# The rows that stream through the later feed-forwards start at other addresses

## Chip, core and metric

One core of a Trainium2 chip runs the whole network in one launch. The metric is the device time of that launch in microseconds (us); the time of the kernel before is the median of three executions, and one further execution was profiled.

## What is computed

The model has two layers over 256 latent tokens and 256 context tokens of width 1024. Each layer is a half-step feed-forward, a token mixer (a two-directional SSD in layer 0, grid pooling in layer 1) and a second half-step feed-forward. The stretch that matters here is the feed-forward on the latent tokens alone, which runs three times: after the mixer of layer 0, before the mixer of layer 1 and after it.

```python
def swiglu(u, wg, wu, wd):
    return (jax.nn.silu(u @ wg) * (u @ wu)) @ wd
...
x = x + 0.5 * m[:, 8] * swiglu(modulate(x, norm_g[i, 2], m[:, 6], m[:, 7]),
                               ffn_w_gate[i, 1], ffn_w_up[i, 1], ffn_w_down[i, 1])
```

The inner width is 2816, that is 22 blocks of 128. All of it is float32.

## The kernel before, in words

Every float32 product is made of three passes through TensorE (`mm3`, L201): a weight tile is split into a high part `hi` and a low remainder `lo`, the activations likewise, and the passes are hi by high rows (L202), lo by high rows (L203) and hi by low rows (L204). The weight block of 128 x 128 is loaded into the array, and the activations are streamed past it: 128 partitions, and along each partition a run of 256 float32 values, one for each token. These runs are the "streamed rows" of this document. Every pass has a weight load of its own.

The last three feed-forwards are one function, `ffn` (L935), called at L1007, L1009 and L1068. Here they are called the first, second and third sub-layer. Each has 22 gate and 22 up tiles (output bank `gu`, rows from the tiles `vh` and `vl`), eight cells of three passes each, and then eight down tiles (output bank `dn`, rows from the 22 pairs `hh` and `hl`), 22 cells of three passes each. In the first NV = 3 gate and up tiles the run is 258 values, since two bias columns ride along while the norm is still being found; from the fourth on (`settle`, L953) and in the down product it is 256.

`vh` and `vl` are [128, 8, 320] tiles of the pool `vp`, one run of 320 values (TS, L335) for each of the eight blocks, of which the slice `c` (L344) picks 258. `Scaled` (L337) makes that slice, and takes its first column from the queue VOFF (L934); it is called four times without tiles of its own, for the first sub-layer (L1003), the second, the pooling mixer and the third (L987, L1042). `hh` and `hl` are 44 tiles of 1024 bytes in a pool that is opened anew in each sub-layer; in front of them `skip` (L110) may reserve some bytes, by the queue HOFF (L995). In the kernel before all offsets are zero.

The layout fixes where these stand. A tile's place is a multiple of 32 bytes: `epsc` (L124), a column of 4 bytes, is followed by `mhalf` 32 bytes on. `vh` begins 145,024 bytes into each partition, `vl` 155,264, the first `hh` 180,864: all three leave 128 when divided by 256, and since a run of `vh` is 1280 bytes and a tile `hh` 1024, so does every streamed run of the three sub-layers. Every weight tile `hi` and `lo` leaves 192, and since a block in it is 512 bytes, so does every loaded block. In the SSD mixer the streamed rows `uh` and `ul` leave 192; in the pooling product `pq` the roles are exchanged, so that the weights' tiles are streamed (192) and `vh` is loaded (128).

The weights come by DMA from SyncE's queue into a ring of six raw tiles (`wsplit`, L190); ScalarE makes `hi`, VectorE `lo`. VectorE also does the modulation products of later layers (L141), whose pace is set at L1002. The order on each engine is the order of the program; the framework puts in the semaphores.

Of the kernel before, what the change touches and what calls it, by code (L numbers as in the profile page):

```python
# [62 lines left out]
def tile_hybrid_backbone(  # L63
# [867 lines left out]
    work = st3.enter_context(tc.tile_pool(name="fw1", bufs=1))  # L931
    adap.append(st3.enter_context(tc.tile_pool(name="ada1", bufs=2)))

    HOFF, VOFF = deque((0, 0, 0)), deque((0, 0, 0, 0))  # L934
    def ffn(l, s, sub, nrm, vec, nxt_vec):  # L935

        ws = [wsplit(wgu[l, s, i % 2, i // 2]) for i in range(2 * NV)]
# [223 lines left out]
```

## Time and profile before

| | us |
|---|---|
| median of three runs | 1321.36 |
| the three runs | 1317.01, 1322.84, 1321.36 |
| the profiled execution | 1321.0 |
| its span, first to last instruction | 1319.1 |
| TensorE busy in the span | 1254.4 |

The profiled execution's own time is 1.9 us over its span, which is the work around it. In the views, PE is TensorE's matmul and PEld its weight load. A matmul's duration in the views (0.28 us for a 256-value run) holds a tail that overlaps the next one; how fast the engine goes is read from the distance of two starts, or from how many matmuls a stretch holds in which the engine is never idle.

### The profile page before, as it was taken

What the parts mean: (1) busy time and instruction counts of PE and PEld (TensorE: products, weight loads), DVE (VectorE), ACT (ScalarE), POOL (GpSimd) and SP (SyncE); (2) the same over time, 40 slices, a digit from 0 to 9 for tenths busy, and PEclk for the clock granted to TensorE, in tenths of its full rate; (3) what the DMA queues carried; (4) which work ended last, traced back from release to release, by engine and by line L of the source; (5) the groups of instructions that cost most, each with busy time, mean ns of one, the idle gap of its engine ahead of it and who ended that gap; (6) DMA issues with size and microseconds to landing.
All of it is one profiled execution on the core that took longest, in us unless ns stands there. A gap on an engine that the chain in (4) does not pass through costs nothing.

```text
span 1319.1 us, 21138 instructions
## 1 busy us (share of the span) xinstructions
PE 1254.4 (95%) x8246; PEld 1120.4 (85%) x8246; DVE 992.4 (75%) x1568; ACT 597.6 (45%) x1023; POOL 177.1 (13%) x121
## 2 busy tenths in 40 slices
PE   4999999989999979899988999999999999999997
PEld 2788888878888757777776999999999999999997
DVE  6889987863367878998997988767987566865553
ACT  3243222222235766655453654544544445745441
POOL 4100000000003141434264300000200000200000
PEclk7999999999999979999999999999999999999999
DMA  9488788872223413434343598777798565275661
GB/s 365 146 303 262 251 329 316 294 268 88 79 89 105 178 48 115 153 119 152 132 153 111 192 332 318 265 214 245 260 318 286 176 192 176 94 242 192 183 186 33
DMA packets 74996, 262.46 MB, mean 199 GB/s; under 512 B 8272, under 2 KB 10768, under 8 KB 73872
## 3 DMA queue, kind: packets, MB, share of 16 engines
q1 hardware_dynamic: 74896, 261.11, 58.5%
q8 instruction: 65, 1.06, 0.3%
q14 instruction: 35, 0.29, 0.1%
HBM read 259.96 MB, written 1.11 MB: 198 GB/s over the span
## 4 chain that ended last, share of the span: by engine, by line
PE 62%; DVE 18%; DMA 8%; issue 4%; ACT 3%; POOL 3%; SPq 1%; POOLq 0%; DVEq 0%; ACTq 0%
PE gu L204 11%; PE gu L202 11%; PE gu L203 11%; PE dn L202 6%; PE dn L204 6%; PE dn L203 6%; DMA adaw<-in_ada_dram 6%; DVE junk L141 6%; DVE lo L198 3%; DVE ca L595 2%; POOL em L708 1%; PE py L768 1%; DMA em<-acd 1%; PE po L772 1%; PE ip L204 1%
## 5 line engine op out<-in xcount | busy, mean ns | idle before, releaser
L198 DVE TENSOR_TENSOR lo<-raw,hi 128x1024 fp32r<-128x1024 f32 (+1 forms) x312 | 386.7, 1242 | 149.8 <-ACT hi L196 149.1
L196 ACT ACTIVATE hi<-raw 128x1024 fp32r<-128x1024 f32 (+1 forms) x333 | 342.8, 1037 | 307.6 <-PE dn L204 123.6
L202 PE MATMUL gu<-vh,hi 128*128 128x256 f32 (+1 forms) x1056 | 295.3, 280 | 3.3 <-DVE sg L967 2.6
L204 PE MATMUL gu<-vl,hi 128*128 128x256 f32 (+1 forms) x1056 | 294.8, 280 | 1.0 <-DVE vl L957 1.0
L203 PE MATMUL gu<-vh,lo 128*128 128x256 f32 (+1 forms) x1056 | 294.9, 279 | 0.0
L141 DVE SCALAR_TENSOR_TENSOR junk<-adaw,cb 128x1024 bf16<-128x1024 f32 x152 | 183.7, 1222 | 48.3 <-DMA adaw<-in_ada_dram 47.6
L202 PE MATMUL dn<-hh,hi 128*128 128x256 f32 (+1 forms) x704 | 215.7, 306 | 4.2 <-DVE x L329 4.2
L204 PE MATMUL dn<-hl,hi 128*128 128x256 f32 (+1 forms) x704 | 215.8, 307 | 0.0
L203 PE MATMUL dn<-hh,lo 128*128 128x256 f32 (+1 forms) x704 | 215.7, 306 | 0.0
L202 PEld LDWEIGHTS gu<-vh,hi 128*128 128x128 f32 x1056 | 199.4, 189 | 3.7 <-DVE sg L967 2.8
L204 PEld LDWEIGHTS gu<-vl,hi 128*128 128x128 f32 x1056 | 200.5, 190 | 1.5 <-DVE vl L957 1.4
L203 PEld LDWEIGHTS gu<-vh,lo 128*128 128x128 f32 x1056 | 199.3, 189 | 0.0
L202 PEld LDWEIGHTS dn<-hh,hi 128*128 128x128 f32 x704 | 132.6, 188 | 11.6 <-issue 4.6
L203 PE MATMUL gu<-uh,lo 128*128 128x512 f32 x352 | 137.8, 392 | 1.9 <-POOL lo L198 1.9
L204 PEld LDWEIGHTS dn<-hl,hi 128*128 128x128 f32 x704 | 133.3, 189 | 6.9
L202 PE MATMUL gu<-uh,hi 128*128 128x512 f32 x352 | 138.6, 394 | 0.0
L203 PEld LDWEIGHTS dn<-hh,lo 128*128 128x128 f32 x704 | 132.5, 188 | 7.0
L204 PE MATMUL gu<-ul,hi 128*128 128x512 f32 x352 | 136.4, 392 | 1.6 <-DVE ul L470 1.4
L243 POOL TENSOR_TENSOR rs<-ms,mhalf 128x2 f32<-128x2 f32 (+1 forms) x6 | 5.4, 904 | 915.9 <-DVE ms L241 915.9
L296 ACT ACTIVATE hh<-hf 128x256 fp32r<-128x256 f32 (+1 forms) x88 | 40.9, 465 | 88.9 <-DVE hf L325 87.0
L203 PEld LDWEIGHTS gu<-uh,lo 128*128 128x128 f32 x352 | 66.4, 189 | 16.2 <-POOL lo L198 2.4
L204 PEld LDWEIGHTS gu<-ul,hi 128*128 128x128 f32 x352 | 65.9, 188 | 15.9 <-DVE ul L470 2.3
(266 smaller groups left out, 1897.5 us busy)
## 6 DMA issues: line engine op xcount, KB each, us to landing
raw<-in_wgu_dram SPq DMA_DIRECT2D x176, 512.0 KB, 4.6
adaw<-in_ada_dram SPq DMA_DIRECT2D x136, 512.0 KB, 5.2
raw<-in_wd_dram SPq DMA_DIRECT2D x64, 512.0 KB, 3.7
raw<-in_win_dram SPq DMA_DIRECT2D x25, 512.0 KB, 3.6
raw<-in_wd_dram SPq DMA_DIRECT2D x32, 384.0 KB, 3.4
raw<-in_wz_dram SPq DMA_DIRECT2D x16, 512.0 KB, 3.6
em<-acd SPq DMA_DIRECT2D x8, 1024.0 KB, 4.8
raw<-in_wout_dram SPq DMA_DIRECT2D x16, 512.0 KB, 4.6
```

What stands on the lines that cost most here:

```text
L141: v.scalar_tensor_tensor(junk, w, 1.0, cb2[i], op0=ALU.mult, op1=ALU.mult, accum_out=M[l][:, t, i : i + 1])
L196: sc.activation(hi[:, 0:n], r[:, 0:n], AF.Copy)
L198: (sub or v).tensor_tensor(lo[:, 0:n], r[:, 0:n], f32(hi[:, 0:n]), op=ALU.subtract)
L202: pe.matmul(out, wh, xh, start=start, stop=False)
L203: pe.matmul(out, wl, xh, start=False, stop=False)
L204: pe.matmul(out, wh, xl, start=False, stop=stop)
L243: gp.tensor_tensor(r, ms, mhalf[:, 0:n], op=ALU.pow)
L296: sc.activation(a, h, AF.Copy)
L595: v.scalar_tensor_tensor(avw[:, :, lo:hi], ov[:, :, lo + off : hi + off], hw[:, 5 * t + k : 5 * t + k + 1], avw[:, :, lo:hi], op0=ALU.mult ...
L708: gp.tensor_tensor(EM[0][:, :, j, :], EM[0][:, :, j, :], EM[1][:, :, j, :], op=ALU.add)
L768: pe.matmul(py[:, hc], EM[0][:, h, j, :], xl[:, hc], start=True, stop=True)
L772: pe.matmul(po, CT[:, j * P : (j + 1) * P], hin[d][0 if j == d else 1], start=True, stop=True)
```

## The change

The two queues of offsets get values, in columns of 4 bytes. No instruction is added, removed or reordered.

```diff
-    HOFF, VOFF = deque((0, 0, 0)), deque((0, 0, 0, 0))
+    HOFF, VOFF = deque((4, 60, 8)), deque((4, 60, 0, 8))
+
     def ffn(l, s, sub, nrm, vec, nxt_vec):
```

In `vh` and `vl` the slice begins 4, 60 and 8 columns in: 16, 240 and 32 bytes. 240 bytes higher is 16 lower, counted in blocks of 256. The pooling mixer's slice stays at 0. In front of `hh` and `hl` the pool gets a reserve of 16, 240 and 32 bytes.

## Rows read from the trace of the kernel before

**Rows 1.** The page: busy time of TensorE; then the chain of waits, 720 us on.
```profile
span 1319.1 us, 21138 instructions
...
PE 1254.4 (95%) x8246; PEld 1120.4 (85%) x8246; DVE 992.4 (75%) x1568; ACT 597.6 (45%) x1023; POOL 177.1 (13%) x121
...
by line: PE gu L204 19.7%; PE gu L202 19.7%; PE gu L203 19.6%; PE dn L202 10.1%; PE dn L204 10.1%; PE dn L203 10.1%; DMA adaw<-in_ada_dram 0.9%; issue 0.7%; PE op L204 0.7%; PE op L203 0.7%; PE op L202 0.7%; PE pq L202 0.6%; DVE x L978 0.5%
```

**Rows 2.** Groups by shape, the whole span: matmuls of 256 and 258, count, mean ns.
```profile
L204 PE MATMUL gu<-vl,hi 128*128 128x256 f32 x912 | 253.6, 278 | 1.0 <-DVE vl L957 1.0
...
L203 PE MATMUL dn<-hh,lo 128*128 128x256 f32 x528 | 146.6, 278 | 0.0
...
L203 PE MATMUL gu<-vh,lo 128*128 128x258 f32 x144 | 41.6, 291 | 0.0
```

**Rows 3.** PE alone in pairs of stretches: first, second, third sub-layer (gate, then down).
```profile
core 0: us, PE busy (x), PEclk, DMA share, GB/s
770.00:850.00 80.00, 80.00 (x709) 1.00 0.90 317
860.00:915.00 55.00, 55.00 (x488) 1.00 0.70 219
950.00:1030.00 80.00, 80.00 (x681) 1.00 0.86 299
1050.00:1105.00 55.00, 55.00 (x469) 1.00 0.64 193
1160.00:1240.00 80.00, 80.00 (x708) 1.00 0.61 201
1250.00:1305.00 55.00, 55.00 (x487) 1.00 0.41 123
```

**Rows 4.** All engines: a stretch of 258-value cells, then the three sub-layers' main stretches.
```profile
core 0: us, PE busy (x) PEld busy (x) DVE busy (x) ACT busy (x) POOL busy (x), PEclk, DMA share, GB/s
922.00:932.00 10.00, 10.00 (x85) 10.00 (x85) 8.25 (x19) 3.33 (x8) 8.86 (x8) 1.00 0.74 250
...
733.00:935.00 202.00, 200.92 (x1746) 200.27 (x1747) 159.41 (x256) 104.73 (x172) 22.22 (x18) 1.00 0.78 263
935.00:1106.00 171.00, 170.22 (x1445) 170.01 (x1444) 121.65 (x177) 84.92 (x127) 0.00 (x0) 1.00 0.74 243
...
1138.00:1310.00 172.00, 171.10 (x1492) 171.02 (x1492) 100.05 (x135) 79.48 (x123) 6.01 (x6) 0.99 0.52 166
```

**Rows 5.** In order of time: the start of the second sub-layer's 256-value runs.
```profile
start us, us, engine line op out<-in xcount [idle before <-releaser]
936.54 0.38 PE L204 MATMUL gu<-vl,hi 128*128 128x256 f32 x1 [0.78 <-DVE vl L957]
936.76 0.28 PE L202 MATMUL gu<-vh,hi 128*128 128x256 f32 x1
...
938.17 0.28 PE L202 MATMUL gu<-vh,hi 128*128 128x256 f32 x1
```

**Rows 6.** In order of time: 256-value runs of the SSD mixer, then of the pooling product.
```profile
630.74 0.28 PE L202 MATMUL ip<-uh,hi 128*128 128x256 f32 x1
...
632.77 0.28 PE L204 MATMUL ip<-ul,hi 128*128 128x256 f32 x1
...
1111.76 0.28 PE L202 MATMUL pq<-hi,vh 128*128 128x256 f32 x1
...
1113.17 0.28 PE L202 MATMUL pq<-hi,vh 128*128 128x256 f32 x1
```

**Rows 7.** In order of time: four weight loads beside one-column matmuls; one load.
```profile
916.52 0.53 PEld L236 LDWEIGHTS nst<-cs,nacc 128*128 128x128 f32 x4
916.63 0.50 PE L236 MATMUL nst<-cs,nacc 128*128 128x1 f32 x4
...
916.96 0.19 PEld L202 LDWEIGHTS gu<-vh,hi 128*128 128x128 f32 x1
```

**Rows 8.** The writers of `vh`, `vl`, `hh`, `hl`: duration min/median/max in ns.
```profile
L956 ACT ACTIVATE vh<-x x24: 401/404/417, 750.7 to 1146.8; 128x256 fp32r<-128x256 f32 x24
L957 DVE TENSOR_TENSOR vl<-x,vh x24: 408/410/421, 752.5 to 1147.4; 128x256 fp32r<-128x256 f32 x24
...
L298 DVE TENSOR_TENSOR hl<-hf,hh x88: 407/418/696, 73.7 to 1251.3; 128x256 fp32r<-128x256 f32 x66, 128x512 fp32r<-128x512 f32 x22
...
L296 ACT ACTIVATE hh<-hf x88: 399/418/636, 72.7 to 1250.3; 128x256 fp32r<-128x256 f32 x66, 128x512 fp32r<-128x512 f32 x22
```

## The prediction

> **What bounds the kernel.** The page's busy times come first: TensorE is busy 1254.4 of 1319.1 us, and in the chain of waits from 720 us on the gate, up and down passes of the three sub-layers hold nearly nine tenths [rows 1]. So a sub-layer's time is the number of its passes times the distance between two starts. The groups by shape give the number: 912 + 528 passes on each of three lines, shared by three sub-layers, which is 1440 passes of 256 values in each, and 144 passes of 258 in each [rows 2].
>
> The stretches of TensorE alone give the distance, and they hold what matters. In all six the engine is never idle and the granted clock is 1.00, that is 2.4 GHz, yet 80 us hold 709 passes in the first sub-layer, 681 in the second and 708 in the third; 55 us of down passes hold 488, 469 and 487 [rows 3]. A stretch counts every pass that touches it, so a pass of 0.28 us adds that much to the length: 80.28 / 709 = 113.2 ns, 80.28 / 681 = 117.9 ns, 80.28 / 708 = 113.4 ns; the down stretches give 113.3, 117.9 and 113.5 ns. **The same instructions on the same addresses run at two paces**, about 113.3 and 117.9 ns, and each sub-layer keeps one from its first 256-value pass to its last. The second sub-layer has its pace from the start: after a stall of 0.78 us, 12 steps from 936.76 to 938.17 us take 117.5 ns each [rows 5].
>
> Nothing else separates the second from its neighbours. Its DMA share is 0.86 where the first has 0.90 at the faster pace [rows 3], and VectorE is busy 121.65 of 171 us there against 159.41 of 202 in the first [rows 4]: 71% and 79%. What is left is how weight loads and streamed rows mesh inside TensorE.
>
> **Do addresses bear on the meshing?** Three relative positions of rows and weights stand in the trace. Where both leave 192 when divided by 256 (SSD mixer), 17 steps from 630.74 to 632.77 us take 119.4 ns each; where the streamed tile stands 64 bytes above the loaded one (pooling product), 12 steps take 1.41 us, 117.5 ns; where it stands 64 below, as in the sub-layers, 113.3 or 117.9 [rows 3, 6]. The slow paces show at every position and the fast one at only one. The first two are stretches of about 2 us, so this is a hint and no more. The change puts the rows 48, 80 and 32 bytes below the weights in gate and up.
>
> The Trainium skill speaks against any effect: "SBUF — State Buffer", section "Who interferes with whom", gives TensorE two independent read ports, one for the moving operand and one for weight loads, and says that TensorE waits on no one. By it the sum is zero and the time 1321. The two paces in one trace show that something in the pair of streams does interfere [rows 3], but not that an address selects it; I give that outcome its own place below.
>
> **Part by part.** Nothing is issued that was not issued before; no DMA, wait or queue is touched.
>
> *Second sub-layer, 16 bytes lower in gate and up.* I take the pace to become the fast one. The pairs of stretches put the difference at 117.9 - 113.4 = 4.5 ns (4.4 to 4.7), and 1440 x 4.5 = 6.5 us. It all lies on the path, as TensorE is never idle. Could the weights follow? The first sub-layer was supplied at that pace with no idle time in the same windows. What is late next is therefore still TensorE. Bounds: nothing gained if it stays slow; a loss of 912 x 3.0 = 2.7 us if its gate and up passes go to the 258-value distance of 10.28 / 85 = 120.9 ns [rows 4].
>
> *First and third, 16 and 32 bytes higher.* They are at the fast pace, and I cost them at nothing. A faster one is hardly there: four weight loads that stand beside one-column matmuls hold 0.53 us, and one load lasts 0.19, so their starts stand (0.53 - 0.19) / 3 = 0.113 us apart [rows 7]: the loads alone go no faster than these passes. Below, each can fall to the slow pace: 6.5 us lost for each.
>
> The Trainium skill has a lower figure: "TensorE: Matmul & The Clock Gate", section "Back-to-back issue gap", gives 262 cycles for 256 columns, by estimate 109.2 ns; by that the three sub-layers could give about 24 us. No row here shows such a pace at 256 values.
>
> *The down product.* The reserve in front of `hh` is rounded up to 32 bytes by the layout, so its rows move by 32, 256 and 32 bytes: in the second sub-layer they stay where they were, counted in blocks of 256. Down passes follow gate passes without idle time and keep their pace in all three [rows 3], so I let them inherit it: of the 6.5 us, 528 x 4.5 = 2.4 hang on this.
>
> *258-value passes.* There are 432 at 120.9 ns. I cost them at nothing; if the run were as cheap by the value as a fast 256 pass (114.2 ns), 432 x 6.7 = 2.9 us would go, and at the far end nothing says that they slow.
>
> *Writers.* ScalarE and VectorE write the shifted rows in 0.40 to 0.42 us each [rows 8]. Were each to take half as long again, 22 pairs in a sub-layer cost 4.6 us on each engine, beside VectorE's idle 21 to 42% [rows 4]: covered, so nothing.
>
> **The sum.** 1321.0 - 6.5 = **1314.5 us** against the profiled execution, which is 0.4 us under the median of the runs, so 0.5% below that median. The three runs spread over 5.8 us, nearly one sub-layer's step, so a sub-layer may well change pace from one execution to the next. A measurement of this kernel can tell about 0.5% from no change, which puts this forecast on the edge.
>
> **Rivals.**
> 1. *Addresses select nothing.* The pace is set by how a stall ends: same addresses, two paces [rows 3, 5]. Against: the three positions [rows 6]. Time: 1321, give or take a sub-layer. (By the port rule of the Trainium skill cited above, this is the case to expect.)
> 2. *Slower: a run that begins off a 64-byte boundary costs what a 258-value run costs.* Two values more cost 120.9 - 113.3 = 7.6 ns where 0.9 would be their share, as if one more part of 64 bytes were begun; a shifted run of 256 values also reaches into one part more. It decides as soon as 16-byte shifts leave the boundary, which all but the second down product do: 2880 x 7.6 + 912 x 3.0 = 24.6 us, 1345.6. Against: the extra could as well come from run lengths that never mesh. The same page of the Trainium skill (section "Door 1: The DMA port swizzle") counts SBUF lines of 16 bytes, and all shifts are multiples of that; no run here shows it.
> 3. *Slower by meshing:* the new positions hold the slow pace in the first and third too. One gives 1327.5 with the second unmended, both 1334.
> 4. *Better:* the second sub-layer gains, and the 258-value passes as well, 1311.6; with a pace in all three under 113 ns, for which I have no row, less still.
>
> **Chances.** The forecast (1312 to 1317) 0.39; rival 4 0.16; rival 1 0.23; rival 3 0.10; rival 2 0.12. Faster by over 0.5% means under 1314.8: rival 4 and two thirds of the forecast, 0.42. Within 0.5% takes the rest of the forecast and rival 1, with a little of rival 3: 0.37. Slower 0.21. The range from 1305 to 1330 leaves out rival 2, half of rival 3 and the far end of rival 4. The forecast's own range is 1312 to 1317.
>
> **What would show it.** In the profile after, 80 us of the second sub-layer's gate passes should hold some 708 passes instead of 681, and 55 us of its down passes 487; the first and third should stand as before; 10 us of 258-value passes should hold 85. Under rival 1 some sub-layer still has 681, or the pattern changes at random from run to run. Under rival 2 every gate stretch holds some 664 (80.28 / 0.1209). The forecast is wrong if the second sub-layer stays at 117.9 ns, if another joins it, or if any stretch goes clearly under 113.

## The result: 0.9% slower, by rows at places against the weights where a pass takes longer

The changed kernel takes 1329.34 us (median of six runs, 1328.23 to 1330.55) where the kernel before takes 1316.58 (six runs, 1309.91 to 1322.84). The ratio is 1.0091, with a 95% interval from 1.0066 to 1.0117. The forecast was 1314.5, with a range from 1305 to 1330: the time lies inside the range, at its very end, and the sign was wrong. The profiled execution of the changed kernel took 1330.2 us with a span of 1328.4. The change adds a blank line at L935, so later lines have numbers one higher than before.

The page, its span and busy times, answers to [rows 1]:

```profile
span 1328.4 us, 21138 instructions
...
PE 1265.3 (95%) x8246; PEld 1132.3 (85%) x8246; DVE 994.8 (75%) x1568; ACT 597.4 (45%) x1023; POOL 177.0 (13%) x121
```

TensorE is 10.9 us longer busy with the same number of instructions. VectorE is 2.4 us longer busy, ScalarE and GpSimd are as they were. Where it is longer busy stands in the stretches of TensorE alone, which answer to [rows 3]; the columns are the stretch, its length, TensorE's busy time and passes, the granted clock, the DMA share and GB/s:

```profile
770.00:850.00 80.00, 80.00 (x673) 1.00 0.85 296
860.00:915.00 55.00, 55.00 (x467) 1.00 0.66 209
950.00:1030.00 80.00, 80.00 (x673) 1.00 0.86 301
1050.00:1105.00 55.00, 55.00 (x487) 1.00 0.65 201
1160.00:1240.00 80.00, 80.00 (x678) 1.00 0.59 196
1255.00:1310.00 55.00, 55.00 (x468) 1.00 0.43 129
```

The rows come in pairs, gate and up first, then down, for the three sub-layers. In them TensorE is never idle and its clock never falls, as before; only the number of passes differs. Worked out as in the prediction, with 0.28 us added to each length, the paces are 119.3 and 118.4 ns in the first sub-layer, 119.3 and 113.5 in the second, 118.4 and 118.1 in the third. Before they were 113.2 and 113.3, 117.9 and 117.9, 113.4 and 113.5 [rows 3]. Five of the six stretches are off the pace of 113.3 ns now. The sixth, the second down product, is the one whose rows the layout's rounding moved by a full 256 bytes.

The differences make 912 x (6.1 + 1.4 + 5.0) = 11.4 us in gate and up and 528 x (5.1 - 4.4 + 4.6) = 2.8 us in down, 14.2 us in all. The span grew by 9.3, because this execution came to the first sub-layer earlier. The change touches nothing that runs before it, and three profiles of the kernel before differ there by as much (shown below with the second experiment). The chain of waits shows the same load of a modulation tile ahead of that sub-layer's norm, here in the kernel before (start, length, what):

```profile
732.75 5.66 DMA adaw<-in_ada_dram
```

and here in the changed kernel:

```profile
728.30 5.84 DMA adaw<-in_ada_dram
```

4.45 us earlier leaves 14.2 - 4.45 = 9.8, and 9.3 were measured.

Two terms that the prediction put at nothing stayed there. Ten microseconds of 258-value passes of the second sub-layer hold 85, as in [rows 4]:

```profile
925.00:935.00 10.00, 10.00 (x85) 10.00 (x84) 8.18 (x19) 2.94 (x9) 8.84 (x8) 1.00 0.68 235
```

and the writers of the shifted rows take what they took in [rows 8]:

```profile
L957 ACT ACTIVATE vh<-x x24: 399/404/419, 746.4 to 1148.8; 128x256 fp32r<-128x256 f32 x24
L958 DVE TENSOR_TENSOR vl<-x,vh x24: 409/414/421, 748.3 to 1149.4; 128x256 fp32r<-128x256 f32 x24
```

Here is the seam between the up tiles and the down product in the second sub-layer of the changed kernel, in order of time:

```profile
1047.62 0.28 PE L203 MATMUL gu<-vh,lo 128*128 128x256 f32 x1
...
1048.21 0.28 PE L202 MATMUL dn<-hh,hi 128*128 128x256 f32 x1
...
1049.59 0.28 PE L202 MATMUL dn<-hh,hi 128*128 128x256 f32 x1
```

Five steps of 0.59 us before the seam are 118 ns each; twelve of 1.38 us after it are 115, on the way to 113.5. There is no idle time at the seam. The pace of the gate and up passes is not carried over to rows that stand at another place.

### The profile page after: what moved, and what is told of

Its sections match the earlier page's. It is cut to its first block, busy times and chain, and to the rows that moved or that the text cites. A ratio compares the mean times of both kernels' runs of the same rounds, so it can differ in the third digit from the quotient of the medians.

```text
span 1328.4 us, 21138 instructions
## 1 busy us (share of the span) xinstructions
PE 1265.3 (95%) x8246; PEld 1132.3 (85%) x8246; DVE 994.8 (75%) x1568; ACT 597.4 (45%) x1023; POOL 177.0 (13%) x121
## 4 chain that ended last, share of the span: by engine, by line
PE 74%; DVE 11%; DMA 6%; ACT 3%; POOL 3%; issue 3%; SPq 0%; POOLq 0%; DVEq 0%; ACTq 0%
PE gu L204 13%; PE gu L202 13%; PE gu L203 13%; PE dn L202 7%; PE dn L204 7%; PE dn L203 7%; DMA adaw<-in_ada_dram 4%; DVE lo L198 2%; DVE junk L141 1%; DVE ca L595 1%; POOL em L708 1%; PE ip L204 1%; PE ip L203 1%; PE py L768 1%; PE ip L202 1%
## 5 line engine op out<-in xcount | busy, mean ns | idle before, releaser
L202 PE MATMUL gu<-vh,hi 128*128 128x256 f32 (+1 forms) x1056 | 299.6, 284 | 3.3 <-DVE sg L968 2.6
L204 PE MATMUL gu<-vl,hi 128*128 128x256 f32 (+1 forms) x1056 | 298.2, 283 | 0.7 <-DVE vl L958 0.7
L203 PE MATMUL gu<-vh,lo 128*128 128x256 f32 (+1 forms) x1056 | 298.1, 283 | 0.0
L323 ACT ACTIVATE sg<-gu 128x256 f32<-128x256 f32 (+1 forms) x79 | 34.9, 442 | 113.9 <-PE gu L204 113.9
```

Source lines behind the costliest of these rows:

```text
L202: pe.matmul(out, wh, xh, start=start, stop=False)
L203: pe.matmul(out, wl, xh, start=False, stop=False)
L204: pe.matmul(out, wh, xl, start=False, stop=stop)
L323: sc.activation(sg, pg, AF.Silu)
```

## The experiments

Two theories were open. **Boundary:** a run of 256 values that begins off a multiple of 64 bytes reaches into one part more and costs 5 to 6 ns. **Relative place:** what counts is where the rows stand against the weights, counted in blocks of 256 bytes, and 64 below is a good place. A third, that no address counts, was rival 1 of the prediction. A stretch of 80, 45, 70 or 35 us is read as above; where TensorE was idle in it, its busy time takes the place of the length.

**The kernel before again.** No edit.

> The kernel before once more, unchanged. Boundary theory (a run of 256 values that begins off a multiple of 64 bytes costs 5 to 6 ns more; one that begins on it is free to settle at 113.3 or 117.8 ns): each sub-layer at 113.3 or 117.8 ns a pass, nothing near 119, and the second sub-layer may well be at 113.3 this time. Rival (the addresses of before fix the pace of each sub-layer): again 113.3, 117.8, 113.3.

It took 1308.8 us, and all its stretches are at the shorter pace:

```profile
765.00:845.00 80.00, 80.00 (x708) 1.00 0.90 316
865.00:910.00 45.00, 45.00 (x400) 1.00 0.71 230
955.00:1025.00 70.00, 68.53 (x604) 1.00 0.84 291
1055.00:1100.00 45.00, 44.88 (x396) 1.00 0.65 206
1160.00:1230.00 70.00, 70.00 (x621) 1.00 0.59 190
1265.00:1300.00 35.00, 33.20 (x293) 1.00 0.14 43
```

That is 113.2 to 114.3 ns in every one, so the 117.9 ns of the second sub-layer in the first profile was not fixed by its addresses. At 64 below the weights two paces are possible. It also shows what can be late next when the second sub-layer runs at the shorter pace. TensorE has 68.53 of 70.00 us busy there, and the view of waits has one, for VectorE's product of gate and up (what waited, for what, us in total, times, longest):

```profile
PE gu L202 <- DVE hf L325: 1.5, 1, 1.5
```

**Gate and up alone.**

```diff
+    HOFF, VOFF = deque((0, 0, 0)), deque((4, 60, 0, 8))
```

> The change in the gate and up rows alone (16, 240, 32 bytes), the down rows where they were. Boundary theory: gate and up at 119.2, 119.2 and 118.3 ns as after the change, down at 113.3 or 117.8 in all three; against all at 113.3 that is 912 x (5.9 + 5.9 + 5.0) = 15.3 us more. Rival (one pace is kept through a whole sub-layer, so down inherits from gate and up): down passes at 118 to 119 ns in all three.

It took 1330.1 us. The gate and up stretches hold 673 in 80 us, 589 and 594 in 70: 119.3, 119.3 and 118.3 ns. The down stretches hold 400, 400 in 45 us and 312 in 35: 113.2, 113.2, 113.1. In the first sub-layer:

```profile
765.00:845.00 80.00, 80.00 (x673) 1.00 0.88 315
865.00:910.00 45.00, 45.00 (x400) 1.00 0.69 220
```

So down does not inherit a pace from gate and up at another place. The gate and up shifts cost 912 x (5.9 + 5.9 + 5.0) = 15.3 us against a kernel with all at 113.3, as expected. The run is 21.3 us longer than the kernel before, run again; another 5.2 lie ahead of the first sub-layer. These are its first passes in the first profile of the kernel before, in the second, and in this run:

```profile
733.04 0.40 PE L202 MATMUL gu<-vh,hi 128*128 128x258 f32 x1 [0.70 <-ACT vh L356]
727.00 0.38 PE L202 MATMUL gu<-vh,hi 128*128 128x258 f32 x1 [0.70 <-ACT vh L356]
732.23 0.39 PE L202 MATMUL gu<-vh,hi 128*128 128x258 f32 x1 [0.70 <-ACT vh L356]
```

With no edit at all, this start moved by 6 us. A time of a whole run therefore doesn't price a place by itself; the stretches do. Both theories say the same of this run.

**Rows and weights together.** Eight columns of reserve ahead of the weight ring move everything behind it by 32 bytes.

```diff
+    wp.tile([P, 8], F32, name="skip", tag="skip", bufs=1)
     stu = ctx.enter_context(ExitStack())
```

> Rows and weights are all moved by 32 bytes together, so that their relative place is that of before, but every run begins off a multiple of 64 bytes. Boundary theory: 118.3 ns a pass in all three sub-layers, gate and down. Rival (the relative place of rows and weights decides): 113.3 or 117.8 ns in each, as before.

It took 1311.9 us, and its stretches are those of the kernel before:

```profile
765.00:845.00 80.00, 78.35 (x689) 1.00 0.88 307
865.00:910.00 45.00, 45.00 (x399) 1.00 0.71 226
...
1055.00:1100.00 45.00, 44.88 (x395) 1.00 0.64 202
1160.00:1230.00 70.00, 70.00 (x620) 1.00 0.59 192
1265.00:1300.00 35.00, 35.00 (x311) 1.00 0.21 65
```

113.4 to 114.3 ns, although every run begins 32 bytes off a multiple of 64. **The boundary theory falls here.**

**Rows 64 bytes higher.**

```diff
+    HOFF, VOFF = deque((16, 16, 16)), deque((16, 16, 0, 16))
```

> All streamed rows of the three sub-layers 64 bytes higher, so that they leave 192 when divided by 256, as the weights do; the runs begin on multiples of 64 bytes. Boundary theory: 113.3 or 117.8 ns. Rival (the relative place of rows and weights decides): another pace, by the 119.4 ns of the SSD mixer's runs at this relative place about 119, in all three.

It took 1338.1 us, the longest of all. All runs begin on multiples of 64 bytes, and no stretch is near 113:

```profile
765.00:845.00 80.00, 80.00 (x669) 1.00 0.86 301
865.00:910.00 45.00, 45.00 (x378) 1.00 0.67 211
...
1160.00:1230.00 70.00, 70.00 (x585) 1.00 0.60 206
1265.00:1300.00 35.00, 35.00 (x294) 1.00 0.64 184
```

119.8 to 120.1 ns throughout (80.28 / 669 = 120.0). That is near the pace of the SSD mixer's short stretch at the same relative place, 119.4 [rows 6].

**Weights alone, 32 bytes lower.** Counted in blocks of 256 bytes, the rows stay: the reserves ahead of the ring move the weights 224 bytes up, which is 32 down in such a block, and those behind it make the rows' move a whole 256.

```diff
+    wp.tile([P, 56], F32, name="skip", tag="skip", bufs=1)
...
-    skip(upool[0], 128)
+    skip(upool[0], 160)
...
-    skip(vp, 192)
+    skip(vp, 224)
```

> The streamed rows stay where they are, the weight tiles of the three sub-layers move 32 bytes down (to 160 when divided by 256), so rows stand 32 below weights as in the changed kernel's third sub-layer. Relative-place theory: 118.3 ns a pass in all three, gate and down. Rival (the rows' own address decides): 113.3 or 117.8 ns, as the rows are untouched.

It took 1334.5 us. The streamed rows have the place in their block that they had, and the pace is that of the changed kernel's third sub-layer, whose rows stand 32 below the weights:

```profile
765.00:845.00 80.00, 80.00 (x678) 1.00 0.90 316
...
1160.00:1230.00 70.00, 70.00 (x594) 1.00 0.62 208
1265.00:1300.00 35.00, 35.00 (x298) 1.00 0.57 166
```

118.4, 118.3 and 118.4 ns. Together with the run that moved both, this settles it for **relative place**: moving the weights does what moving the rows does, and moving both leaves the pace as it was.

**A map of the places.** Four kernels, in this order, put the three sub-layers at other places. The first moves the down rows too; the other three leave them at -64.

```diff
+    HOFF, VOFF = deque((40, 56, 24)), deque((32, 48, 0, 24))
...
+    HOFF, VOFF = deque((0, 0, 0)), deque((1, 2, 0, 62))
...
+    HOFF, VOFF = deque((0, 0, 0)), deque((20, 28, 0, 36))
...
+    HOFF, VOFF = deque((0, 0, 0)), deque((12, 44, 0, 52))
```

The last two also moved the first feed-forward's rows, by other reserves in front of its tiles (`skip` of 192 and 256 in place of 128 at L364, with more ahead of `wp0`, `hid` and `scp`).

> Gate and up rows 128, 192 and 96 bytes higher, down rows 160, 224 and 96 higher: six stretches, rows at +64, +128, +32 against the weights in gate and up, +96, -96, +32 in down. Relative-place theory: one fixed pace for each stretch, the two stretches at +32 alike (118 to 120 ns), +64 about 117.5 as in the pooling product; if some place is under 113.3 ns it shows here. Rival (only -64 is ever fast): all six at 117 to 121 ns.

> Gate and up rows 4, 8 and 248 bytes higher (8 lower), down untouched. If the place matters to the byte, 118 to 119 ns already at 4 bytes; if it matters in steps of 16 bytes, 4 and 8 bytes higher stay at 113.3 and 8 lower goes to 119.3 as 16 lower did. Down at 113.3 or 117.8.

> Gate and up rows of the three sub-layers at +16, +48 and +80 bytes against the weights, down untouched; the first feed-forward's rows (512 values) at +64 in gate and up and +128 in down. Relative-place theory: each stretch at one fixed pace between 117.5 and 121 ns, down at 113.3 or 117.8; 512-value passes at one fixed pace each, 226.7 or 233.3 ns by the two places known. A stretch under 113.3, or 512-value passes under 226.7, would be a better place than any so far. Rival (128 different multiples of 16 bytes do not matter, only multiples of 64 do): +16, +48 and +80 alike at 120.0.

> Gate and up rows at -16, +112 and -112 bytes against the weights, down untouched; the first feed-forward's rows at +128 in gate and up and +32 in down. Relative-place theory: each stretch at one fixed pace between 117.5 and 121 ns, down at 113.3 or 117.8; the 512-value passes at +128 in gate and up at the pace that +128 has in the down product of the run beside this one. Rival (gate and down differ by more than the place): another pace there.

They took 1329.7, 1325.6, 1327.9 and 1327.3 us. The expected 117.5 to 121 ns missed at three places, +112, +16 and -16, which are quicker. With the runs above, the pace of a 256-value pass by the place of the rows against the weights (bytes, in blocks of 256), from the stretches:

| place | ns | place | ns | place | ns |
|---|---|---|---|---|---|
| -112 | 118.7 | -56 | 119.9 | +32 | 117.9 |
| -96 | 118.5 | -48 | 119.3 | +48 | 118.3 |
| -80 | 119.3 | -32 | 118.4 | +64 | 117.9 |
| -72 | 119.9 | -16 | 117.2 | +80 | 118.5 |
| -64 | 113.2 or 117.9 | 0 | 120.0 | +96 | 119.8 |
| -60 | 120.0 | +16 | 116.7 | +112 | 113.2 to 113.9 |
| | | | | +128 | 118.7 |

Four bytes off the place at -64 already cost 6.8 ns, in the fine map's first sub-layer, the first line here; the second line is the same sub-layer's down product, left where it was:

```profile
765.00:845.00 80.00, 80.00 (x669) 1.00 0.87 307
865.00:910.00 45.00, 45.00 (x400) 1.00 0.71 225
```

Sixteen-byte steps are not the unit, then. The rival that only multiples of 64 matter falls too: +16 stands at 116.7 ns, +48 and +80 at 118.3 and 118.5, none at 120.0, and +112 is as good a place as -64, as the second sub-layer of the last map shows (1.7 us of idle time in it):

```profile
955.00:1025.00 70.00, 68.26 (x602) 1.00 0.88 307
```

A block of 256 bytes is the right unit as far as the runs go: places 128 apart have different paces (-112 and +16, -16 and +112), and the blocks of one product, whose places differ by multiples of 256, all go at one pace.

Down at -64 stood at 113.2 to 113.5 ns in eight of the nine stretches that were left there (three in each of the last three kernels) and at 117.9 in one, the first sub-layer of the run with +16 (384 in 45 us).

**The first feed-forward's rows, 64 bytes lower.** Its runs have 512 values and stand at the weights' own place.

```diff
-    skip(upool[0], 128)
+    skip(upool[0], 64)
...
+        skip(wp0, 64)
...
-        skip(scp, 128)
+        skip(scp, 192)
```

> Rows of the first feed-forward (512 values a run, at the weights' own place, 226.7 ns a pass) moved 64 bytes down, to the place that is fast in the later ones; the SSD mixer's input rows move with them, all else stays. If each weight load costs the row stream the same at 512 values as at 256, a pass goes from 226.7 by 120.0 - 113.3 = 6.7 ns to 220.0, over 1056 + 504 passes 10.4 us. Rival (a 512-value run has room for the load and the place is of no account): 226.7 ns and the time of before.

It took 1322.4 us. The expectation was wrong, and so was its rival: the place counts for 512-value runs, and between these two places it is the other way round. In this kernel 70 us of gate and up passes of the first feed-forward hold 301 (its down passes, not moved, are the second line):

```profile
195.00:265.00 70.00, 70.00 (x301) 1.00 0.89 317
285.00:310.00 25.00, 25.00 (x112) 1.00 0.51 175
```

and in the kernel before, run again, 311:

```profile
195.00:265.00 70.00, 70.00 (x311) 1.00 0.90 318
285.00:310.00 25.00, 25.00 (x112) 1.00 0.39 130
```

A 512-value pass lasts 0.39 us (393 ns in the page's groups); with that for the pass at the edge it is 233.9 against 226.3 ns. Place 0, among the worst for 256 values, is the best seen for 512; the maps' kernels held 308 passes at +64 and 301 at +128 there.

In the third sub-layer of this run, which was not touched, 597 passes in 70 us (117.7 ns) show the other pace of -64 once more. Its start bears on rival 1, by which a stall sets the pace. The first two lines are its last 258-value pass and its first 256-value one:

```profile
1140.68 0.28 PE L204 MATMUL gu<-vl,hi 128*128 128x258 f32 x1
1140.80 0.28 PE L202 MATMUL gu<-vh,hi 128*128 128x256 f32 x1
...
1142.21 0.28 PE L202 MATMUL gu<-vh,hi 128*128 128x256 f32 x1
```

Twelve steps of 1.41 us, 117.5 ns each, and no idle time ahead of them: a sub-layer can take the longer pace without a stall. The down product at 117.9 ns in the run with +16 also began without one.

**A version with +112.** Gate and up of all three sub-layers at the second good place.

```diff
+    HOFF, VOFF = deque((0, 0, 0)), deque((44, 44, 0, 44))
```

> Gate and up rows 176 bytes higher in all three sub-layers (+112 bytes against the weights), the second place found at 113.3 ns; down untouched. If +112 is a place that always settles fast, gate and up at 113.3 in all three and a time like the best of before, about 1309, in every run: ratio 0.995 to 1.0 against a kernel before whose runs fall between 1309 and 1323. Rival (two paces there as at -64): a sub-layer at about 117.8 now and then, and no difference from before.

It took 1310.38 us (median of 12 runs, 1308.68 to 1315.79), the kernel before beside it 1314.91 (17 runs, 1309.52 to 1327.18): ratio 0.9955, interval 0.9924 to 0.9986. So it is 0.45% faster than the kernel before, and its slowest run is quicker than every run of the changed kernel. Its gate and up stretches:

```profile
765.00:845.00 80.00, 80.00 (x709) 1.00 0.91 316
955.00:1025.00 70.00, 70.00 (x620) 1.00 0.85 293
1160.00:1230.00 70.00, 70.00 (x620) 1.00 0.59 191
```

113.2, 113.4 and 113.4 ns. The best runs of both are alike, and the spread is smaller. That +112 never settles at a longer pace is not shown, since its 12 runs have one profile.

**The kernel before a third time.** No edit.

> The kernel before for the third time. Every sub-layer at 113.3 or 117.8 ns a pass in gate, up and down; which of them is slow, if any, may differ from the two profiles so far (117.8 in the second; none). Its time follows: 1309 with none, about 6.4 us more for each that is slow.

It took 1308.4 us, and its gate and up stretches hold 708 in 80 us, 620 in 70 and 620 in 70, its down stretches 400 in 45 us, 395 in 44.89 and 290 in 33.08: 113.2 to 115.0 ns, and none is at the longer pace. Its first sub-layer began at 726.9 us. In four profiles of rows at -64 in gate and up (three of the kernel before, one of the run that moved the first feed-forward) two of twelve sub-layers were at 117.8 ns, and with the run that moved everything two of fifteen. In all fifteen the down product, at -64 as well, had the pace of gate and up.

## Why the prediction was wrong

**What bounds the kernel** held: the time of these sub-layers is the number of passes times the distance of two starts, and what the change cost was found there. 1440 passes in each, and TensorE's clock at 1.00 in all stretches, were right. One reading was a little off: the first sub-layer did not have its pace from the first pass. After a stall at 754.20 us, six steps from 754.43 to 755.13 took 117 ns each before the 113 began.

**The question about addresses** is where it failed. The prediction had the three relative places in hand, 119.4, 117.5 and 113.3 or 117.9 ns [rows 3, 6], called them a hint, and then let the three new places have the 113.3 ns of the old one. The step "I take the pace to become the fast one" for the second sub-layer had no row behind it: 113.3 had been seen at one place only, and both places that were not that one had shown 117 to 120. Taken at their word, the same rows price the change: five of six stretches at 117.5 to 119.4 ns, the sixth where it was.

**Second sub-layer, -6.5 us.** In its place stand 912 x 1.4 = +1.3 us in gate and up and 528 x -4.4 = -2.3 in down. The down gain can't be put down to the change: its rows kept their place, and the kernel before reaches that pace there by itself in two of three profiles.

**First and third, nothing.** This is the term that the result turns on. Each lost: 912 x 6.1 + 528 x 5.1 = 8.3 us and 912 x 5.0 + 528 x 4.6 = 7.0 us. The floor of 113 ns under them, from the loads alone [rows 7], was never passed by any place, so that bound held. (The estimate of 109.2 ns worked out from the Trainium skill, "TensorE: Matmul & The Clock Gate", section "Back-to-back issue gap", which gives its 262 cycles for a single matmul's gap, was not reached either: 113.1 is the least of any stretch.)

**Down inherits the pace of gate and up:** wrong for rows at another place, where down takes its own pace with no idle time at the seam. Where both stood at -64 the two agreed in all fifteen sub-layers, so the rows that the prediction read couldn't tell. That the reserve is rounded to 32 bytes, so that the second down product stays in place, was right and is visible in the result.

**258-value passes and writers** at nothing: right in the stretch and the group shown.

**The rivals.** Rival 3, meshing at a longer pace in the first and third, was nearest to what happened, given 0.10; its 1334 took the longer pace of -64 (117.9) for both and left the second unmended. Rival 2 had the sign but not the cause, and 7.6 ns a pass where 4.6 to 6.1 were measured: runs that begin off a multiple of 64 bytes are as quick as any when the weights move with them. Rival 1 has a point at -64, where one place has two paces, but a stall isn't needed for the longer one, and elsewhere the place selects. The rule of the Trainium skill that it cited ("SBUF — State Buffer", section "Who interferes with whom": two independent read ports, TensorE waits on no one) does not predict this pair of streams: with the rows where they were in their blocks, moving the weights took a pass from 113.3 to 118.4 ns.

**The reference point** was off as well. The one profile of before that the sum was made against had a sub-layer at 117.9 ns, and it came to the first sub-layer 6 us later than the two others. In those two all three were at 113.3, and against those the change's profiled execution is 1330.2 - 1308.6 = 21.6 us longer; 15.3 in gate and up and 528 x (5.1 + 4.8) = 5.2 in down account for 20.5, and a start of the first sub-layer 1.5 us later covers the rest. That the measured time still fell inside the range is luck: the range's upper end stood for one more sub-layer at the longer pace, while five stretches went to paces longer still.

What stays open is why -64 and +112 are good places, and what decides at -64 between 113.3 and 117.8 ns. That some runs of the kernel before reach 1327 would fit all three sub-layers at the longer pace (1308.6 + 3 x 6.4 = 1328), or two of them and a late start of the first (1308.6 + 2 x 6.4 + 6 = 1327); no profile shows either. Why the first sub-layer starts up to 6 us later in some executions is open as well.

## What to carry to other kernels

Where each pass has a weight load of its own and the runs are short, read the distance between starts, not the busy time, and treat the place of the streamed rows against the weight tiles as a parameter: 4 bytes were worth 6%. A tile added or resized between the two can move it, while one in front of both left the pace alone here, so check the pace after edits that only touch the layout, and choose the place for each run length by itself, since the best place seen for 512 values was among the worst for 256. A pace that occurs at one place only is evidence for that place, not a state that other places may also reach.

## What the runs showed of the hardware

At 2.4 GHz a 256-value pass in float32 took from 113.3 to 120.0 ns by the relative address of two operands alone, with the granted clock at 1.00 in all these stretches, and at one place (rows 64 bytes below the weights) it kept one of two paces through a whole sub-layer of some 165 us. 512-value passes took from 226.3 to 233.9 ns in the same way. Moving rows and weights together by 32 bytes left the pace as it was.
